# Another engine for the feature stores, a softmax taken in steps, a later swap of y, and four more gather buffers with a new pace in the routed stage of a PEER block

## The chip, the core and the metric

The kernel runs on one core of one Trainium2 chip. The metric is device time in microseconds (us) of one execution. A core has five engines, each with its own instruction stream, worked off in order: TensorE (PE, matrix products), VectorE (DVE), ScalarE (ACT), GpSimd (POOL) and SyncE (SP, which here only issues DMAs). Engines wait for each other by semaphores; DMA transfers are issued into a queue by one of the engines and move between HBM (DRAM) and the on-chip memories SBUF and PSUM.

## The reference, cut to what matters

The program is one layer of a hybrid decoder block for 256 tokens of width 2048: sparse attention and a convolution group side by side, an output projection, a residual with LayerNorm that gives y, and then a PEER mixer with 16384 experts, a second residual and a LayerNorm. The change lies in the PEER mixer:

```python
q = (yb @ wq).reshape(bsz, PEER_BLOCK, PEER_HEADS, 2, PK_HALF)
s1 = jnp.einsum('bthd,hkd->bthk', q[..., 0, :], sub_keys[:, 0])
s2 = jnp.einsum('bthd,hkd->bthk', q[..., 1, :], sub_keys[:, 1])
v1, i1 = lax.top_k(s1, PK_TOPK)
v2, i2 = lax.top_k(s2, PK_TOPK)
...
top, pos = lax.top_k(cand, PK_TOPK)
eidx = jnp.take_along_axis(cidx, pos, axis=-1)
g = jax.nn.softmax(top.astype(jnp.float32), axis=-1)
u = u_tab[eidx]
v = v_tab[eidx]
h = jax.nn.gelu(jnp.einsum('btd,bthkd->bthk', yb, u))
return jnp.einsum('bthk,bthkd->btd', g * h, v).astype(y.dtype)
```

Every token has 8 heads with 16 experts each, so 128 (head, rank) pairs a token, chosen among 128 x 128 experts (index = i1 * 128 + i2). `u_tab` and `v_tab` have 16384 rows of 2048 floats. For every pair the row of `u_tab` is multiplied with y, and the row of `v_tab` is added to the output with weight g * gelu(that product).

## The kernel before, in words

**Two ways to the same product.** The 256 tokens are two halves (tt = 0 and 1) of 128, one token on each partition. The columns of `u_tab` are split. The last 896 columns (`UG`) are fetched row by row: an indirect gather on GpSimd's queue (`gather_to`, L1168) brings, for one pair number c of one half, 128 rows of 896 floats, one for each token, and one VectorE instruction (`dot`, L1179) multiplies them with y and sums them into a column of `hv`. There are 256 such gathers, 128 for each half; `issued` counts gathers and `done` counts dots. The first 1152 columns (`UD`, nine chunks of 128) are computed densely: all 16384 experts are multiplied with y by TensorE, whichever are needed.

**The dense u loop (L1613 on).** Block j (of 128) takes 128 experts. `u_load` (L1208) has SyncE load them into one of four buffers `ur`. `u_split` makes two parts of them: ScalarE rounds them to the high part `uh` (L1232) and copies the first 768 columns to PSUM (`ut`, L1236); VectorE subtracts for the low part (L1237), GpSimd does it for the rest (L1238). `u_mult` is 27 matmuls on the block's transposed experts (high by high L1515, high by low L1516, low by high L1519) into one of two PSUM tiles, and `u_keep` (L1522) evicts these to `W[:, :, j]` by ScalarE. The loop body is an order written out by hand. For block j: the load for j + 4, the matmuls of j, the eviction of j - 1, the split of j + 2, then `dots_until`, which issues gathers up to a due count (at most two, `CATCH`, more than there were), and does the dots whose buffers it needs for them; then one step of `later_steps` (two, if the routing is behind the gathers).

**y and its swap.** The y that the dots read is a copy in PSUM, `yp`, of one half. When gather 128, the first of half 1, is about to be issued, `fetch` (L1489) reads y of half 1 into one of the gather buffers, by GpSimd's queue. The first `dot` of half 1 calls `swap` (L1495): ScalarE copies that buffer to `yp`.

**Routing in steps.** `later_steps` is a generator. It goes through the top-k selection of all heads, and then through `feature_steps`: for i1 and i2 VectorE makes four feature rows (`fr`: a constant, the index, and its square taken apart), each a bf16 tile of 128 x 256 in one of four scratch buffers, and ScalarE issues the ten stores that put them in DRAM (`feats`). Behind them stands the softmax of the gates, `gate_softmax`, once for each half: subtract (L1138, VectorE), exponent (L1139, ScalarE), sum, reciprocal and product (L1140 to L1142, VectorE). Two transposes by TensorE (L1562) and a copy give the gates' transposed form `gT`.

**The routed stage (L1652 to the v stage).** It picks, from `W`, the dense results for the experts that each token has chosen, and puts the weights back into `W` at the same places. A step q (of 64) does four tokens. Steps 0 to 35 go in pairs: `ext_hot` and `ext_mask` (L1660 and L1669, small matmuls from the stored features), a ReLU by ScalarE (`ext_relu`, L1665), four matmuls with `W` a step (`ext`, L1674; fp32, which the records count as eight), and a maximum by VectorE (`ext_max`, L1678). Steps 36 to 64 do one q each and also scatter block m = q - 37: `sc_hot`, `sc_relu`, `sc_val`, four matmuls `sc` (L1722) and `sc_keep`. The last 28 blocks are only scattered, in pairs. Around q = 32 the sums of half 0 are completed: `weight_sums` (after step 32), `weight_gelu` (ScalarE), `weight_gates` (L1693, VectorE, at step 34), and `weight_rows` (a transpose, L1653 in `to_cols`, into bank 4 and a copy, L1696, at step 36).

**Gathers and dots in the routed stage.** At its start 200 gathers were issued and 197 dots done. The other 56 go into spare buffers: three 896-column pieces of what held the transposed y (`more`), and the ring's three buffers as their dots are done. `x_dots(q, n)` is called behind each step's `ext`: gathers are issued up to the due count n; if no buffer is spare, the next dot is done. For every third dot (i % 3 == 1) the product alone goes to GpSimd (L1836), in place, and ScalarE sums it with an accumulating copy (`x_sum`, L1846) when a call at least two steps later comes to it; only then is the buffer spare again. In the last eight steps one more dot a step is done.

**After it** the v stage multiplies `W` with `v_tab`, dense and gathered in the same manner (L296 to L298 and L1745).

Of the kernel before, what the change touches and what calls it, by code (L numbers as in the profile page):

```python
# [8 lines left out]
F32 = mybir.dt.float32  # L9
# [4 lines left out]
AF = mybir.ActivationFunctionType  # L14
# [5 lines left out]
P = 128  # L20
# [59 lines left out]
def tile_hybrid_block(  # L80
# [1052 lines left out]
        for _ in route_steps(h, tt):  # L1133
            pass

    def gate_softmax(tt):
        sh = [P, PH, TOPK]
        nc.vector.tensor_tensor(gs[:, tt], top[:, tt], top[:, tt, :, 0:1].to_broadcast(sh), op=OP.subtract)  # L1138
        nc.scalar.activation(gs[:, tt], gs[:, tt], AF.Exp)  # L1139
        nc.vector.tensor_reduce(gsum[:, tt, :, 0], gs[:, tt], axis=AX.X, op=OP.add)  # L1140
        nc.vector.reciprocal(gsum[:, tt], gsum[:, tt])
        nc.vector.tensor_tensor(gs[:, tt], gs[:, tt], gsum[:, tt].to_broadcast(sh), op=OP.mult)  # L1142

    def fl(t, tt):
        return t[:, tt].rearrange("p a b -> p (a b)")
# [25 lines left out]

    def dot(i):
        tt, c = pairs[i]
        if yrow["tt"] is not None and yrow["tt"] != tt:
            yrow["swap"](tt)
        gt, ring = gts.pop(i)
        ring[2] -= 1
        yr = yg[:, tt, HC - UG:] if yrow["tt"] is None else yrow["at"]
        nc.vector.scalar_tensor_tensor(gt, gt, 1.0, yr, op0=OP.mult, op1=OP.mult,  # L1179
                                       accum_out=hv[:, tt, c:c + 1])  # L1180
# [31 lines left out]
    def dots_until(n, ending=10 ** 6):  # L1212
        nonlocal issued, done
        while issued < n:
            last = issued >= ending
            if issued == P:
                while rings[0][2] == rings[0][1]:
                    dot(done)
                    done += 1
                yrow["fetch"](1)  # L1220
            while room() == 0 or (last and rings[0][2] == rings[0][1]):
                dot(done)
                done += 1
            gather(issued, last)
            issued += 1
# [270 lines left out]
        rings[0][2] -= 1  # L1496
        yrow["tt"] = tt

    yrow["swap"], yrow["fetch"] = swap, fetch

    wpool = ctx.enter_context(ExitStack())
    wp = wpool.enter_context(tc.tile_pool(name="wp", bufs=1, reuse_waits="tile"))
# [25 lines left out]
    def feature_steps():  # L1528
        dump("i1", i1)
        dump("i2", i2)  # L1530
        for n, src in enumerate((i1, i2)):

            size = BIGM if n == 0 else 1.0
            v = src.rearrange("p a b c -> p a (b c)")
            sqf = tk.tile([P, 2, P], F32, name=f"fsq{n}", tag="oh", bufs=1)
            nc.vector.tensor_tensor(sqf, v, v, op=OP.mult)
            sqi = tk.tile([P, 2, P], U32, name=f"fsi{n}", tag="cand", bufs=1)
            nc.vector.tensor_copy(sqi, sqf)
            yield
            for f in range(4):  # L1540
                fr = tk.tile([P, 2, P], BF, name=f"fr{n}{f}", tag="scr", bufs=4)
                if f == 0:
                    nc.vector.memset(fr, size)
                elif f == 1:
                    nc.vector.tensor_scalar(fr, v, size, None, op0=OP.mult)
                else:
                    si = tk.tile([P, 2, P], U32, name=f"fi{n}{f}", tag="oh", bufs=1)
                    if f == 2:
                        nc.vector.tensor_scalar(si, sqi, 7, 7, op0=OP.logical_shift_right,
                                                op1=OP.logical_shift_left)  # L1550
                    else:
                        nc.vector.tensor_scalar(si, sqi, 127, None, op0=OP.bitwise_and)
                    nc.vector.tensor_scalar(fr, si, size, None, op0=OP.mult)
                yield
                for r in ((0, 1) if f == 0 else (f + 1,)):
                    nc.scalar.dma_start(feats[n][:, r].rearrange("a p c -> p a c"), fr)
        for tt in range(2):
            gate_softmax(tt)
            yield
        pt = psu.tile([P, UV], F32, name="colsg", tag="ut", bufs=2)  # L1560
        for tt in range(2):
            nc.tensor.transpose(pt[:, tt * P:(tt + 1) * P], fl(gs, tt), ident)  # L1562
        nc.scalar.activation(gT, pt[:, :T], AF.Copy)
        yield
# [47 lines left out]
    if True:  # L1612
        for j in range(P):  # L1613
            if j == P - 2:
                for _ in steps:
                    pass
                first_loads()
            upto = min(first + (rest - LATE) * (j + 1) // P + GAHEAD, 2 * P)
            if j + URB < P:
                u_load(j + URB)  # L1620
            u_mult(j)
            if j:
                u_keep(j - 1)
            if j + 2 < P:
                u_split(j + 2)
            dots_until(min(upto, routed, issued + CATCH), ending)
            next(steps, None)
            if routed < min(upto + 8, 2 * P):
                next(steps, None)
        for _ in steps:  # L1630
            pass
        assert not rings[1][2]
        rings.pop()
# [11 lines left out]

    xs = ctx.enter_context(ExitStack())
    px = xs.enter_context(tc.tile_pool(name="px", bufs=2, reuse_waits="tile"))

# [43 lines left out]

    def weight_rows(tt):
        nc.scalar.activation(wv[:, tt], to_cols(wT[:, tt * P:(tt + 1) * P], f"wvT{tt}",  # L1696
                                                more_banks[0] if tt else 4), AF.Copy)

    ohs, oas, pos = {}, {}, {}

# [130 lines left out]
    def x_dot(q):  # L1831
        nonlocal done
        i, done = done, done + 1
        gt, ring = gts[i]
        if i % 3 == XPOOL and i0 <= i < 2 * P - 4:
            nc.gpsimd.tensor_tensor(gt, gt, yx, op=OP.mult)  # L1836
            late.append((q, i))
            return
# [9 lines left out]

    def x_dots(q, n):
        nonlocal issued  # L1850
        while late and late[0][0] <= q - 2:
            x_sum()
        while issued < n:
            while not spare:
                if done < issued:
                    x_dot(q)
                else:
                    x_sum()
            gather_to(issued, spare.pop(0), [None, 0, 0])
            issued += 1  # L1860
        if q > NQ - 8 and done < issued:
            x_dot(q)

    manual = ctx.enter_context(ExitStack())
    manual.enter_context(tc.manual_schedule())
    if True:
        for q, hp in enumerate([ext_hot(q, True, 4) for q in range(2)]):
            ext_relu(q, hp, True)
        u_left = 2 * P - issued
        i0 = issued  # L1870

        def due(q):
            pace = q + 1 + PACE * max(0, q - LAG)
            return min(2 * P, i0 + -(-u_left * pace // (NQ - 4 + PACE * (NQ - 4 - LAG))))

        def loads(q):
            m = q - LAG
# [29 lines left out]
        for q in range(QP, NQ + 1):  # L1907
# [33 lines left out]
                sc_keep(m, sc(m) if q < NQ else sp)  # L1941
            if q == NQ:
                weight_gelu(1)
            if q == QP:
                weight_rows(0)
        for m in range(NQ - QP, NQ, 2):
            loads(m + LAG)
            loads(m + LAG + 1)
# [9 lines left out]
            sps = [sc(p, True) for p in (m, m + 1)]  # L1958
            for p, sp in zip((m, m + 1), sps):
                sc_keep(p, sp, p % 2 == 1)  # L1960
            if m == NQ - 12:
                v_raw(2)
                v_rows(0, 0)
# [5 lines left out]
            if m == NQ - QP + 4:  # L1969
                weight_rows(1)  # L1970
            if m == NQ - QP + 2:
                tks.close()
                upool.close()
                keep.close()
# [187 lines left out]
```

## Time and profile before

| | us |
|---|---|
| runs shown (3) | 1589.81, 1589.48, 1586.29 |
| median | 1589.48 |
| the profiled execution | 1588.19 |
| its span, first to last instruction | 1586.4 |

| stretch of the profiled execution | us | TensorE | VectorE | ScalarE | GpSimd | clock | DMA share |
|---|---|---|---|---|---|---|---|
| attention, convolution, y, query scores (0 to 507) | 507 | 499.30 | 393.09 | 269.18 | 228.56 | 1.00 | 0.59, then 0.70 |
| dense u loop (507 to 915) | 408 | 401.10 | 378.99 | 298.08 | 297.18 | 1.00 | 0.99 |
| routed stage, steps 0 to 64 (915 to 1038) | 123 | 113.82 | 104.82 | 79.09 | 94.11 | 0.94 | 0.75 |
| scatter alone (1038 to 1078) | 40 | 39.96 | 32.67 | 36.13 | 27.31 | 1.00 | 0.57 |
| v stage to the end (1078 to 1586) | 508 | 496.64 | 457.43 | 216.94 | 397.10 | 1.00 | 0.95 |

The columns of engines are busy times in us. "Clock" is the TensorE clock that the throttle granted, 1.00 being full speed, and "DMA share" is the mean busy share of the 16 DMA engines. The page of the profile lists groups of instructions by source line, with how often they ran, their mean time, how long the engine stood idle just before them, and which other engine's work ended that. `fr` is a feature row, `ur` a block of experts, `yp` y in PSUM, `gu`, `spare`, `moreh` and `morel` are gather buffers, `top` also holds the extracted activations `ha`, and `gs` the gates and later the weights. In a line with `->` or `<-` the part left of the arrow is written, and behind `<-` in brackets stands what the instruction waited for and for how long.

### The profile page before, as it was taken

The page shows a single profiled execution, that of the slowest core. Times are in us where ns is not written, and L with a number is a line of the kernel's source. Part 1 is how long each engine was busy: PE and PEld are TensorE (multiplying, and loading weights), DVE is VectorE, ACT ScalarE, POOL GpSimd, SP SyncE. Part 2 cuts the span into 40 slices and gives each one's busy share as a digit, 9 for nine tenths or more (in the row PEclk, how much of TensorE's full clock was granted, in tenths as well). Part 3 has the DMA queues.
Part 4 walks back from the last instruction along what each step waited for, and adds up shares of the span by engine and source line. Part 5 has one row for each costly group of instructions (what it writes and reads, how often), then busy time and mean ns, then how long its engine had stood idle before and what let it go on. Part 6 is the DMA issues. An engine that isn't in the chain of part 4 may idle for free.

```text
span 1586.4 us, 29450 instructions
## 1 busy us (share of the span) xinstructions
PE 1550.8 (98%) x10987; PEld 1435.9 (91%) x10987; DVE 1367.0 (86%) x2509; ACT 899.4 (57%) x1266; POOL 1044.3 (66%) x791
## 2 busy tenths in 40 slices
PE   9999999999999999999998999999999999999997
PEld 9999999988999999999998977788888888888886
DVE  6999777766578999999997788888999989989998
ACT  5345776645435777777776656785444444444443
POOL 1886000064887777777776677867888878878883
PEclk9999999999999999999999999999999999999999
DMA  9774455255867999999999886767999999999997
GB/s 299 239 231 147 139 161 184 92 207 182 258 209 272 397 382 393 383 390 384 387 388 366 304 276 216 235 196 247 346 368 355 356 371 346 357 376 355 366 356 248
DMA packets 161896, 466.59 MB, mean 294 GB/s; under 512 B 18304, under 2 KB 86424, under 8 KB 161496
## 3 DMA queue, kind: packets, MB, share of 16 engines
q1 hardware_dynamic: 117188, 261.95, 47.8%
q0 software_dynamic: 41040, 201.82, 34.5%
q8 instruction: 86, 1.41, 0.4%
q10 hardware_dynamic: 3524, 0.95, 0.3%
q14 instruction: 58, 0.48, 0.1%
HBM read 459.80 MB, written 4.85 MB: 293 GB/s over the span
## 4 chain that ended last, share of the span: by engine, by line
PE 83%; DVE 7%; DMA 3%; POOL 3%; issue 2%; ACT 2%; POOLq 0%; ACTq 0%; DVEq 0%
PE f L297 10%; PE f L298 10%; PE f L296 10%; PE hp L1515 8%; PE hp L1516 8%; PE hp L1519 7%; PE bank L1722 3%; DVE taps L492 2%; PE pwq L298 2%; PE pwq L297 2%; PE pwq L296 2%; PE bank L1674 2%; DMA feat<-fr 1%; PE mixa L296 1%; PE pcg L297 1%
## 5 line engine op out<-in xcount | busy, mean ns | idle before, releaser
L1745 POOL DMA_INDIRECT gv<-in_peer_v_dram,e x256 | 400.5, 1565 | 91.1 <-DVE gacc L1750 48.3
L1785 ACT ACTIVATE vh<-vr 128x1408 fp32r<-128x1408 f32 (+1 forms) x129 | 175.8, 1364 | 274.8 <-DVE gacc L1750 230.9
L297 PE MATMUL f<-vl,wh 128*128 128x512 f32 (+1 forms) x768 | 288.3, 375 | 1.7 <-DVE vl L1786 1.7
L296 PE MATMUL f<-vh,wh 128*128 128x512 f32 (+1 forms) x768 | 288.5, 376 | 0.0
L298 PE MATMUL f<-vh,wl 128*128 128x512 f32 (+1 forms) x768 | 288.1, 375 | 0.0
L1515 PE MATMUL hp<-yh,uh 128*128 128x256 f32 x1152 | 283.8, 285 | 4.2 <-ACT W L1522 4.2
L1516 PE MATMUL hp<-yl,uh 128*128 128x256 f32 x1152 | 283.4, 284 | 0.0
L257 POOL TENSOR_TENSOR lo<-raw,hi 128x1024 fp32r<-128x1024 f32 (+1 forms) x84 | 189.0, 2271 | 133.9 <-ACT hi L239 127.8
L1168 POOL DMA_INDIRECT gu<-in_peer_u_rows_dram,e x200 | 193.6, 968 | 117.9 <-DVE gu L1179 72.0
L1786 DVE TENSOR_TENSOR vl<-vr,vh 128x1408 fp32r<-128x1408 f32 (+1 forms) x129 | 206.5, 1602 | 41.3 <-ACT vh L1785 39.9
L1515 PEld LDWEIGHTS hp<-yh,uh 128*128 128x128 f32 x1152 | 222.5, 193 | 4.8 <-ACT W L1522 4.8
L1516 PEld LDWEIGHTS hp<-yl,uh 128*128 128x128 f32 x1152 | 222.6, 193 | 0.0
L1179 DVE SCALAR_TENSOR_TENSOR gu<-gu,yp 128x896 f32<-128x896 f32 x200 | 211.2, 1080 | 12.2 <-DMA gu<-in_peer_u_rows_dram,e 12.2
L239 ACT ACTIVATE hi<-raw 128x1024 fp32r<-128x1024 f32 (+1 forms) x137 | 141.2, 1036 | 141.0 <-PE pcg L297 29.1
L1750 DVE SCALAR_TENSOR_TENSOR gacc<-gv,hv,gacc 128x640 f32<-128x640 f32 x247 | 207.4, 880 | 2.9 <-DMA gv<-in_peer_v_dram,e 2.8
L1232 ACT ACTIVATE uh<-ur 128x1152 fp32r<-128x1152 f32 x128 | 149.6, 1168 | 95.6 <-issue 69.3
L297 PEld LDWEIGHTS f<-vl,wh 128*128 128x128 f32 x768 | 148.8, 194 | 22.9 <-DVE vl L1786 2.4
L296 PEld LDWEIGHTS f<-vh,wh 128*128 128x128 f32 x768 | 148.8, 194 | 20.7
L298 PEld LDWEIGHTS f<-vh,wl 128*128 128x128 f32 x768 | 149.0, 194 | 19.5
L1519 PE MATMUL hp<-yh,ul 128*128 128x256 f32 x1152 | 159.3, 284 | 0.0
L1519 PEld LDWEIGHTS hp<-yh,ul 128*128 128x128 f32 x1152 | 147.6, 192 | 0.1
L1237 DVE TENSOR_TENSOR ul<-ut,uh 128x768 fp32r<-128x768 f32 x126 | 119.9, 952 | 26.1 <-ACT ut L1236 23.2
(407 smaller groups left out, 3491.6 us busy)
## 6 DMA issues: line engine op xcount, KB each, us to landing
vr<-in_peer_v_dram SPq DMA_DIRECT2D x128, 704.0 KB
ur<-in_peer_u_dense_dram SPq DMA_DIRECT2D x128, 576.0 KB
raw<-in_w_in_dram SPq DMA_DIRECT2D x32, 1024.0 KB
raw<-in_w_out_dram SPq DMA_DIRECT2D x16, 1024.0 KB
raw<-in_peer_wq_dram SPq DMA_DIRECT2D x15, 1024.0 KB
gv<-in_peer_v_dram,e POOLq DMA_INDIRECT x256, 7.4
gu<-in_peer_u_rows_dram,e POOLq DMA_INDIRECT x200, 6.5
raw<-in_w_in_dram SPq DMA_DIRECT2D x4, 608.0 KB
```

The source lines that it names most:

```text
L257: e.tensor_tensor(lo[:, a:b], src[:, a:b], hi[:, a:b].bitcast(F32), op=OP.subtract)
L296: nc.tensor.matmul(acc, lhsT=ah, rhs=bh, start=start, stop=False)
L297: nc.tensor.matmul(acc, lhsT=ah, rhs=bl, start=False, stop=False)
L298: nc.tensor.matmul(acc, lhsT=al, rhs=bh, start=False, stop=stop)
L1168: nc.gpsimd.indirect_dma_start(out=gt, out_offset=None, in_=u_rows, in_offset=bass.IndirectOffsetOnAxis(ap=fl(e4, tt)[:, c:c + 1], axis=0))
L1179: nc.vector.scalar_tensor_tensor(gt, gt, 1.0, yr, op0=OP.mult, op1=OP.mult, accum_out=hv[:, tt, c:c + 1])
L1515: nc.tensor.matmul(hps[j], lhsT=uh[:, s], rhs=chunk(yh, k), start=k == 0, stop=False)
L1516: nc.tensor.matmul(hps[j], lhsT=uh[:, s], rhs=chunk(yl, k), start=False, stop=False)
L1519: nc.tensor.matmul(hps[j], lhsT=ul[:, s], rhs=chunk(yh, k), start=False, stop=k == UK - 1)
L1745: nc.gpsimd.indirect_dma_start(out=gvs[j, tt], out_offset=None, in_=v_tab, in_offset=bass.IndirectOffsetOnAxis(ap=fl(e4, tt)[:, j:j + 1], ...
L1750: engine.scalar_tensor_tensor(gacc[:, tt], gvs.pop((j, tt)), wv[:, tt, j:j + 1], gacc[:, tt], op0=OP.mult, op1=OP.add)
L1786: (nc.gpsimd if early else nc.vector).tensor_tensor(vl, src[:, s], vh.bitcast(F32), op=OP.subtract)
```

## The change

It has two parts.

In the dense u loop: the ten stores of the features are issued by SyncE instead of ScalarE. `gate_softmax` becomes a generator over both halves at once: a subtraction, two steps of pause, the exponent, one step of pause, then sum, reciprocal and product, and two more steps of pause before the transposes. `dot` no longer swaps y. `dots_until` returns when the dots of half 0 are all done and y hasn't been swapped; the swap is called in the loop body, behind the split of block j + 2 and ahead of `dots_until`.

In the routed stage: four more buffers of 896 columns (pool `gx`) are spare from the start, and are given back after the second pair of the last part. `x_dots` counts dots against the due count, not gathers; the count starts from the dots done (197) and is spread over nearly all 64 steps. All spare buffers are filled with gathers behind the dots of each call, as long as there are gathers left. The sum of a product is taken four steps after it instead of two. Products for GpSimd are counted in `owed`, and those that fall on steps 32 to 34 are put off to a later dot. The extra dot in the last eight steps goes. `weight_rows(0)` moves from step 36 to the second pair of the last part, and into bank 5.

```diff
-    def gate_softmax(tt):
-        sh = [P, PH, TOPK]
-        nc.vector.tensor_tensor(gs[:, tt], top[:, tt], top[:, tt, :, 0:1].to_broadcast(sh), op=OP.subtract)
-        nc.scalar.activation(gs[:, tt], gs[:, tt], AF.Exp)
...
+    def gate_softmax():
+        sh = [P, 2 * PH, TOPK]
+        g3, t3, s3 = (t.rearrange("p a b c -> p (a b) c") for t in (gs, top, gsum))
+        nc.vector.tensor_tensor(g3, t3, t3[:, :, 0:1].to_broadcast(sh), op=OP.subtract)
+        yield
+        yield
+        nc.scalar.activation(g3, g3, AF.Exp)
+        yield
+        nc.vector.tensor_reduce(s3[:, :, 0], g3, axis=AX.X, op=OP.add)
+        nc.vector.reciprocal(s3, s3)
+        nc.vector.tensor_tensor(g3, g3, s3.to_broadcast(sh), op=OP.mult)
+        yield
+        yield
...
     def dot(i):
         tt, c = pairs[i]
-        if yrow["tt"] is not None and yrow["tt"] != tt:
-            yrow["swap"](tt)
+        assert yrow["tt"] in (None, tt)
...
             while room() == 0 or (last and rings[0][2] == rings[0][1]):
+                if done == P and yrow["tt"] == 0:
+                    return
                 dot(done)
                 done += 1
...
                 for r in ((0, 1) if f == 0 else (f + 1,)):
-                    nc.scalar.dma_start(feats[n][:, r].rearrange("a p c -> p a c"), fr)
-        for tt in range(2):
-            gate_softmax(tt)
-            yield
+                    nc.sync.dma_start(feats[n][:, r].rearrange("a p c -> p a c"), fr)
+        yield from gate_softmax()
...
             if j + 2 < P:
                 u_split(j + 2)
+            if done == P and yrow["tt"] == 0:
+                swap(1)
             dots_until(min(upto, routed, issued + CATCH), ending)
...
+    gxs = ctx.enter_context(ExitStack())
+    gx = gxs.enter_context(tc.tile_pool(name="gx", bufs=1, reuse_waits="tile"))
+    spare.extend(gx.tile([P, UG], F32, name=f"gx{n}") for n in range(4))
...
     def weight_rows(tt):
         nc.scalar.activation(wv[:, tt], to_cols(wT[:, tt * P:(tt + 1) * P], f"wvT{tt}",
-                                                more_banks[0] if tt else 4), AF.Copy)
+                                                more_banks[0] if tt else 5), AF.Copy)
...
-        if i % 3 == XPOOL and i0 <= i < 2 * P - 4:
+        owed["n"] += i0 <= i < 2 * P - 4 and i % 3 == XPOOL
+        if owed["n"] and i0 <= i and not NQ // 2 <= q < NQ // 2 + 3:
+            owed["n"] -= 1
             nc.gpsimd.tensor_tensor(gt, gt, yx, op=OP.mult)
             late.append((q, i))
             return
...
     def x_dots(q, n):
         nonlocal issued
-        while late and late[0][0] <= q - 2:
+        while late and late[0][0] <= q - 4:
             x_sum()
-        while issued < n:
-            while not spare:
-                if done < issued:
-                    x_dot(q)
-                else:
+        while done < n:
+            while done == issued:
+                if not spare:
                     x_sum()
+                gather_to(issued, spare.pop(0), [None, 0, 0])
+                issued += 1
+            x_dot(q)
+        while spare and issued < 2 * P:
             gather_to(issued, spare.pop(0), [None, 0, 0])
             issued += 1
-        if q > NQ - 8 and done < issued:
-            x_dot(q)
...
-        u_left = 2 * P - issued
-        i0 = issued
+        u_left = 2 * P - done
+        i0, d0, owed = issued, done, {"n": 0}

         def due(q):
             pace = q + 1 + PACE * max(0, q - LAG)
-            return min(2 * P, i0 + -(-u_left * pace // (NQ - 4 + PACE * (NQ - 4 - LAG))))
+            return min(2 * P, d0 + -(-u_left * pace // (NQ - 1 + PACE * (NQ - 2 - LAG))))
...
-            if q == QP:
-                weight_rows(0)
...
+            if m == NQ - QP + 2:
+                weight_rows(0)
...
             if m == NQ - QP + 2:
+                gxs.close()
```

More of the change, by code (lines that the diff above doesn't have):

```diff
@@ L1134, in route @@
             pass
-    def gate_softmax(tt):
-        sh = [P, PH, TOPK]
[L1138 to L1142, printed above, removed]
+    def gate_softmax():
[11 more added lines that the diff above has]
+        yield
     def fl(t, tt):
@@ L1497, in swap @@
         yrow["tt"] = tt
-    yrow["swap"], yrow["fetch"] = swap, fetch
+    yrow["fetch"] = fetch
     wpool = ctx.enter_context(ExitStack())
```

## The prediction

> **What bounds the kernel now.** I read the page first, then the chain of waits over the expert half, then the waits and timelines of the places where that chain leaves TensorE.
>
> ```profile
> span 1586.4 us, 29450 instructions
> PE 1550.8 (98%) x10987; PEld 1435.9 (91%) x10987; DVE 1367.0 (86%) x2509; ACT 899.4 (57%) x1266; POOL 1044.3 (66%) x791
> PE 83%; DVE 7%; DMA 3%; POOL 3%; issue 2%; ACT 2%; POOLq 0%; ACTq 0%; DVEq 0%
> ```
>
> TensorE sets the end. The profiled execution took 1588.19 us (span 1586.4 and 1.8 around it), 0.1% under the median of the three runs, 1589.48. A gain can only come from the 17% of the chain that is not PE, and from matmuls slowed by waiting. The change touches two stages.
>
> In the dense u loop one block is 768+384 columns, 27 matmuls and one eviction W (L1522). The chain shows its period and two breaks:
>
> ```profile
> 735.59 1.08 PE hp L1519 x9
> 738.83 1.08 PE hp L1519 x9
> ...
> 759.95 1.08 PE hp L1519 x9
> ...
> 834.47 1.08 PE hp L1519 x9
> ...
> 839.27 17.17 DMA feat<-fr
> ...
> 874.76 1.08 PE hp L1519 x9
> ```
>
> The evictions of these two stretches, counted by stretch (columns: stretch, length, busy and count, clock, DMA share, GB/s):
>
> ```profile
> 738.83:759.95 21.12, 3.76 (x6) 1.00 0.99 365
> 834.47:874.76 40.29, 6.26 (x10) 0.96 0.99 361
> ```
>
> The undisturbed period is 738.83 - 735.59 = 3.24 us. The first stretch, with y's swap, lost 21.12 - 6 x 3.24 = 1.68 us; the second, with feature stores and the gates' softmax, 40.29 - 10 x 3.24 = 7.89. So 9.57 us is all that the edits in this loop can return. The waits that made them, ScalarE's and one of TensorE's:
>
> ```profile
> ACT yp L1495 <- DVE gu L1179: 1.8, 1, 1.8
> ACT W L1522 <- DMA feat<-fr: 5.3, 2, 3.6
> ACT gs L1139 <- DVE gs L1138: 3.7, 2, 3.3
> PE colsg L1562 <- DVE gs L1142: 2.5, 1, 2.5
> ```
>
> ScalarE is in order: each time it stands for a swap, a store or an exponent, the next high part and the eviction stand behind it, and TensorE stops.
>
> In the routed stage (L1674 rebuilds hidden activations, L1722 scatters weights) the period is that of the first two rows here; the others are its first pair, the pairs q = 32 and 34, and q = 63:
>
> ```profile
> 976.88 1.16 PE L1674 MATMUL bank<-W,slot 128*128 128x128 f32 x8
> 979.19 1.05 PE L1674 MATMUL bank<-W,slot 128*128 128x128 f32 x7
> ...
> 912.59 2.05 PE L1674 MATMUL bank<-W,slot 128*128 128x128 f32 x16
> 954.35 2.05 PE L1674 MATMUL bank<-W,slot 128*128 128x128 f32 x16
> 957.79 2.05 PE L1674 MATMUL bank<-W,slot 128*128 128x128 f32 x16
> 1034.63 1.16 PE L1674 MATMUL bank<-W,slot 128*128 128x128 f32 x8
> ```
>
> A pair of blocks (first half) and a block with a scatter (second) both want 2.31 us. 17 pairs took 45.20 where 39.27 would do, the 28 blocks after them 76.84 where 64.68 would do: 18.1 us lost. GpSimd is nearly as busy, by its products and gathers from 915.9 to 1031:
>
> ```profile
> 915.90:1031.00 115.10, 35.60 (x17) 0.94 0.76 240
> 915.90:1031.00 115.10, 54.53 (x57) 0.94 0.76 240
> ```
>
> and by the pitch of its queue:
>
> ```profile
> 919.53 0.95 POOL L1168 DMA_INDIRECT moreh<-in_peer_u_rows_dram,e  x1 [0.30 <-issue]
> 920.79 0.95 POOL L1168 DMA_INDIRECT morel<-in_peer_u_rows_dram,e  x1 [0.30 <-issue]
> ...
> 930.27 2.08 POOL L1836 TENSOR_TENSOR morel<-morel 128x896 f32<-128x896 f32 x1
> 932.51 0.98 POOL L1168 DMA_INDIRECT spare<-in_peer_u_rows_dram,e  x1 [0.16 <-DVE top L1678]
> ```
>
> A gather takes 1.25 us of the queue, a product 2.25: 57 x 1.25 + 17 x 2.25 = 109.5 of 115.1 us. TensorE's 18 us are therefore not all to be had.
>
> **The u loop, edit by edit.** *Swap.* The copy of 0.92 us moves behind the next block's high part, one step after the last dot that reads the old y, so its wait of 1.8 us is over before ScalarE comes to it.
>
> ```profile
> 756.02 0.92 ACT L1495 ACTIVATE yp<-yrow 128x896 f32<-128x896 f32 x1 [1.75 <-DVE gu L1179]
> 831.31 1.17 ACT L1232 ACTIVATE uh<-ur 128x1152 fp32r<-128x1152 f32 x1 [0.82 <-issue]
> 863.60 1.28 ACT L1139 ACT_TABLE_LOAD   x1 [0.91 <-DVE fr L1553]
> ```
>
> ScalarE idles 0.82 us a step, so 0.92 leaves about 0.1. VectorE's dots of that step, and the gathers that the early return puts off, wait behind the copy; catching up at two a step covers them. Gain 1.5, bounds 0.7 (the copy wholly uncovered) to 1.68.
>
> *Softmax.* One chain of five VectorE and ScalarE instructions on both halves replaces two; the exponent runs two steps after the subtraction and the reduction a step after that, the transposes two steps later. So 3.7 on ScalarE and 2.5 on TensorE go. The table load of 1.28 stays, with about 0.4 of exponent: 1.7 against 0.82 of slack, and two PSUM banks for the block's sums to carry the rest. I leave 0.3 us lost, bounds 0 and 0.9.
>
> *Stores.* Ten stores leave ScalarE, with the 5.3 us that it waited. SyncE now waits for each feature row; queued behind are the u loads, and ScalarE's high part waits for those.
>
> ```profile
> 834.60 0.33 SPq L1208 DMA_DIRECT2D ur<-in_peer_u_dense_dram  x1
> ...
> 836.15 0.41 DVE L1545 TENSOR_SCALAR fr<-i 128x256 bf16<-128x256 f32 x1
> ...
>   DMA ur<-in_peer_u_dense_dram: 0.9, 1
> ```
>
> A load that left at 834.60 would now leave behind a row ready at 836.56: 2 us late. Loads have that much in hand: of 128 high parts one waited for its load, 0.9 us (last row). I leave 1.0 us lost; its bounds are 0 and the price in the second rival.
>
> The loop: 1.68 - 1.5 = 0.18 and 1.3 of 7.89 stay, so 8.1 us are gained.
>
> **The routed stage.** Four more buffers mean that the queue on GpSimd no longer waits for a free one, but also that at q = 0 eight gathers are put into it at once instead of one. By the code's own order the first product (dot 202) stood behind 8 gathers since number 200 and was read by ScalarE (x_sum) at q = 13; now it stands behind 12 and is read at q = 11. The fifth product (214) stood behind 20 gathers and was read at q = 31; now 24, read at q = 29. From 919.53 (gather 201) the first product starts at 919.53 + 11 x 1.25 = 933.3 instead of 930.27; the fifth at 933.3 + 12 x 1.25 + 4 x 2.25 = 957.3, is done at 959.4, and with ScalarE's sum (1.1, estimated from the 896 columns of the copy above) the ReLU behind it feeds pair 32 at 961 instead of 954.35. ScalarE already stood for these products:
>
> ```profile
> ACT morel L1846 <- POOL morel L1836: 5.1, 2, 2.7
> ```
>
> The longer lag (four q instead of two) doesn't cover it, since the product is issued four to five q earlier in the order too. Dots 197 and 198 also come ahead of the first reductions on VectorE, which already waited for a gather:
>
> ```profile
> 916.92 1.09 DVE L1179 SCALAR_TENSOR_TENSOR gu<-gu,yp 128x896 f32<-128x896 f32 x1 [2.37 <-DMA gu<-in_peer_u_rows_dram,e]
> ```
>
> That is 2 to 3 us more for TensorE at the third pair, but inside the hold just worked out.
>
> At the turn to the second half three waits lie together:
>
> ```profile
> 959.07 2.22 DVE L1693 TENSOR_TENSOR gs<-top,i 128x128 f32<-128x128 f32 x1 [1.04 <-ACT top L1689]
> ...
> 959.04 2.09 POOL L1836 TENSOR_TENSOR moreh<-moreh,morel 128x896 f32<-128x896 f32 x1
> ...
> 963.97 0.47 PE L1653 MATMUL bank<-ident,gs 128*128 128x128 f32 x1 [2.42 <-DVE top L1678]
> ```
>
> The gate product on VectorE lasted just as long as GpSimd's product beside it; no product is issued at q = 32 to 34 now, and the transposes of L1653 move to the last part, where they cost TensorE the same 0.3 to 0.5 us. So 2.42 goes; the Gelu's table load (1.28 as above) and the sum of dot 217 stay ahead of q = 36 on ScalarE, which I put at 968. From there GpSimd is ahead: by the order of the code every product is done before its sum, so 27 blocks at 2.31 end at 1030.4. I add 2 us for slow matmuls behind the remaining stops: 1032.4 against 1034.63, a gain of 2.2. Bounds: GpSimd's floor, 915.9 + 109.5 = 1025.4 and a sum and a block after it, 1027.5 (7.1 gained); and the 6.6 of pair 32 kept to the end (6.6 lost). I take 2.2, from the row of the queue.
>
> The 2 us are from this row, the stretch with the stop of 2.42:
>
> ```profile
> 960.00:970.00 10.00, 7.39 (x38) 5.09 (x36) 7.09 (x11) 3.98 (x9) 6.10 (x5) 0.66 0.65 214
> ```
>
> The granted clock was 0.66 in it. [...]
>
> **Sum.** 1588.19 - 8.1 - 2.2 = 1577.9; I forecast 1578 for the median. The runs differ by 3.5 us among themselves, so 0.2% (3.2 us) is what a measurement can tell from no change: faster is under 1586.3, slower over 1592.7.
>
> **Rivals.** *GpSimd is no hold (0.20).* If ScalarE comes to the sums late enough, TensorE follows GpSimd's floor: 7.1 in the stage and 9 in the loop give 1572. For it: GpSimd waited for buffers before, and these waits are what the change removes. Against: the order puts more gathers ahead of each product.
>
> *Stores starve the loads (0.15).* [...]
>
> *The hold lasts (0.18).* The first half's 6.6 us is not made up: 1588.2 - 8.1 + 6.6 = 1586.7, and 1590 with another 3 us of slow clock.
>
> **How the numbers follow.** Forecast 0.47, between 1573 and 1583. Faster: 0.47 + 0.20 + 0.08 of the third rival = 0.75. Same: 0.06 of the second and 0.07 of the third. Slower: 0.09 and 0.03 = 0.12. The range runs from below the GpSimd floor, 1569, to 1590, which leaves out most of the starved loads and the tail of the best case.
>
> **What would show it.** In the changed profile the u loop has no break near 751 or 850 longer than 0.5 us, no ScalarE wait for feat, and the high parts wait for ur under 2 us in all. In the routed stage gathers follow each other at 1.25 without waits for dots, products start later than before up to q = 30 and earlier after q = 38, and L1674 is behind before's at q = 32 and ahead at q = 63. I am wrong if ScalarE doesn't wait for the products at all, if ur is waited for by more than 5 us, or if the gain lies in neither stage.

## The result

| | median us | ratio to before [95% interval] |
|---|---|---|
| kernel before, 6 runs | 1589.64 | |
| the change, 6 runs | 1580.76 | 0.9946 [0.9933, 0.9958] |

The change makes the kernel 0.54% faster, 8.9 us in the medians. The forecast was 1578.0 and the case behind it 1573 to 1583. The profiled execution of the change took 1580.19 us, 8.0 less than that of before. Its page:

```profile
span 1578.4 us, 29466 instructions
PE 1547.6 (98%) x10987; PEld 1433.3 (91%) x10987; DVE 1363.7 (86%) x2505; ACT 898.4 (57%) x1265; POOL 1041.5 (66%) x791
PE 86%; DVE 6%; DMA 2%; issue 2%; POOL 2%; ACT 1%; POOLq 0%; SPq 0%; DVEq 0%; ACTq 0%
```

TensorE is still what ends last; its share of the chain rose from 83 to 86%, and VectorE, the DMAs and GpSimd gave up the rest. Where the 8.0 us lie is read from four stretches that begin and end with the same instructions in both kernels: the six blocks of the u loop with y's swap, the fifteen blocks with the features and the softmax, and the routed stage from step 0 to 36 and from 36 to 63. The columns are the stretch, its length, TensorE's busy time and count, its clock, DMA share and GB/s. First before, then the change:

```profile
738.66:759.78 21.12, 19.87 (x164) 1.00 0.99 364
834.30:890.79 56.49, 51.02 (x409) 0.97 0.96 346
912.59:960.39 47.80, 44.49 (x362) 1.00 0.85 273
960.39:1034.63 74.24, 68.73 (x534) 0.91 0.71 225
```

```profile
738.59:759.67 21.08, 19.83 (x164) 1.00 0.95 356
834.19:885.02 50.83, 49.21 (x410) 1.00 1.02 390
906.82:962.45 55.63, 47.46 (x362) 0.91 0.85 282
962.45:1026.22 63.77, 63.41 (x534) 0.97 0.70 223
```

The swap's six blocks are as long as before (six periods of 3.24 are 19.44). The fifteen blocks lost 56.49 - 15 x 3.24 = 7.89 us and lose 50.83 - 48.60 = 2.23 now. The routed stage first falls back by 55.63 - 47.80 = 7.8 us and then makes up 74.24 - 63.77 = 10.5. So 5.7 us come from the loop and 2.6 from the stage, and what follows takes 0.4 longer.

**The swap.** ScalarE's row of it in the changed kernel:

```profile
755.90 0.92 ACT L1502 ACTIVATE yp<-yrow 128x896 f32<-128x896 f32 x1 [1.75 <-DVE gu L1184]
```

It is the row of before with other line numbers, 1.75 us of wait and all. In ScalarE's order of instructions the copy stands where it stood, behind the same `ut` and ahead of the same eviction.

**Stores and softmax.** No wait of ScalarE for a feature or for the subtraction is left. Its waits for u loads, 0.9 us before, are these now, and the rows after them are where TensorE's last break begins:

```profile
ACT uh L1239 <- DMA ur<-in_peer_u_dense_dram: 7.6, 6, 1.9
```

```profile
861.86 1.17 ACT L1239 ACTIVATE uh<-ur 128x1152 fp32r<-128x1152 f32 x1 [1.92 <-DMA ur<-in_peer_u_dense_dram]
...
865.32 1.17 ACT L1239 ACTIVATE uh<-ur 128x1152 fp32r<-128x1152 f32 x1 [1.03 <-DMA ur<-in_peer_u_dense_dram]
...
867.20 1.28 ACT L1142 ACT_TABLE_LOAD   x1
868.50 0.42 ACT L1142 ACTIVATE gs<-gs 128x256 f32<-128x256 f32 x1
```

Two late loads use up ScalarE's slack, the table load and the exponent come on top, and TensorE loses 1.87 us at block 117 and 0.35 at block 119.

**The routed stage.** VectorE at the third pair, then TensorE:

```profile
911.44 1.09 DVE L1184 SCALAR_TENSOR_TENSOR gu<-gu,yp 128x896 f32<-128x896 f32 x1 [2.17 <-DMA gu<-in_peer_u_rows_dram,e]
...
913.44 1.09 DVE L1184 SCALAR_TENSOR_TENSOR gu<-gu,yp 128x896 f32<-128x896 f32 x1 [0.91 <-DMA gu<-in_peer_u_rows_dram,e]
```

```profile
916.34 1.18 PE L1679 MATMUL bank<-quad,fext 20*128 20x512 bf16 x2 [4.84 <-DVE top L1688]
```

The dots that are now due from step 0 wait for gathers that the loop issued late; the maxima behind them on VectorE hold the banks (of PSUM, into which TensorE writes), and TensorE stops for 6.0 us against 2.4 before. At step 14 it stops again, for the first product:

```profile
927.80 0.95 POOL L1174 DMA_INDIRECT moreh<-in_peer_u_rows_dram,e  x1 [0.30 <-DVE gx L1184]
928.77 2.10 POOL L1848 TENSOR_TENSOR morel<-morel 128x896 f32<-128x896 f32 x1
...
930.90 0.95 ACT L1858 ACTIVATE morel<-morel 128x896 f32<-128x896 f32 x1 [3.93 <-POOL morel L1848]
```

At the turn to the second half the gate product on VectorE, which took 2.22 us in before beside a product of GpSimd, is short with none beside it:

```profile
961.14 0.29 DVE L1703 TENSOR_TENSOR gs<-top,i 128x128 f32<-128x128 f32 x1 [1.13 <-ACT top L1699]
```

From step 38 on there is no stop left: the 25 steps from 38 (at 968.50) to 63 (at 1026.22) take 57.72 us, 25 periods of 2.31.

### The profile page after: what moved, and what is told of

The parts are those of the page before. It is cut to its first block, busy times and chain, and to the rows that moved or that the text cites. A ratio compares the mean times of both kernels' runs of the same rounds, so it can differ in the third digit from the quotient of the medians.

```text
span 1578.4 us, 29466 instructions
## 1 busy us (share of the span) xinstructions
PE 1547.6 (98%) x10987; PEld 1433.3 (91%) x10987; DVE 1363.7 (86%) x2505; ACT 898.4 (57%) x1265; POOL 1041.5 (66%) x791
## 4 chain that ended last, share of the span: by engine, by line
PE 86%; DVE 6%; DMA 2%; issue 2%; POOL 2%; ACT 1%; POOLq 0%; SPq 0%; DVEq 0%; ACTq 0%
PE f L297 10%; PE f L298 10%; PE f L296 10%; PE hp L1522 8%; PE hp L1523 8%; PE hp L1526 8%; PE bank L1732 3%; PE bank L1684 3%; DVE taps L492 2%; PE pwq L298 2%; PE pwq L297 2%; PE pwq L296 2%; PE mixa L296 1%; DMA ur<-in_peer_u_dense_dram 1%; PE pcg L297 1%
```

## The experiments

All runs are read with the same four stretches. "Lost" is the stretch less its periods. The stretches are those of one profiled execution of each kernel, those of before and of the change as above. The first four ran on one chip, the next four on a second, the last four on a third; the kernel before took 1594.5, 1588.4 and 1589.4 us there, and the ratios are to it.

| kernel | ratio [95% interval] | swap lost | features lost | steps 0 to 36 | steps 36 to 63 |
|---|---|---|---|---|---|
| before | 1 | 1.68 | 7.89 | 47.80 | 74.24 |
| the change | 0.9946 [0.9933, 0.9958] | 1.64 | 2.23 | 55.63 | 63.77 |
| e1 loop's edits alone | 0.9972 [0.9955, 0.9988] | 1.64 | 3.68 | 51.83 | 73.76 |
| e2 stage's edits alone | 1.0052 [1.0029, 1.0075] | 1.76 | 7.47 | 58.02 | 69.15 |
| e3 stores on ScalarE | 1.0028 [1.0009, 1.0046] | 1.64 | 0.56 | 59.58 | 67.76 |
| e4 swap later | 1.0019 [0.9998, 1.0041] | 0.13 | 6.04 | 58.97 | 68.65 |
| e5 the change again | 0.9935 [0.9909, 0.9961] | 1.64 | 3.52 | 55.39 | 63.78 |
| e6 aged rows | 0.9935 [0.9916, 0.9955] | 1.83 | 1.05 | 55.27 | 62.19 |
| e7 late dots | 0.9912 [0.9886, 0.9937] | 1.66 | 2.03 | 51.28 | 62.85 |
| e8 fewer products | 0.9942 [0.9924, 0.996] | 1.64 | 2.88 | 56.06 | 62.11 |
| e9 stage's edits alone | 0.9957 [0.994, 0.9973] | 1.64 | 11.05 | 55.40 | 61.93 |
| e10 late dots, swap, ScalarE | 0.9914 [0.9881, 0.9946] | 0.14 | 3.87 | 50.95 | 62.96 |
| e11 late dots, swap, aged rows | 0.9886 [0.9855, 0.9917] | 0.13 | 1.04 | 50.83 | 62.83 |
| e12 no buffers | 0.9954 [0.9942, 0.9966] | 1.63 | 1.31 | 50.82 | 69.97 |

**The two halves of the change, e1, e2 and e9.** e1 is before with the loop's edits, e2 and e9 are one kernel: the change with these undone.

```diff
...
-                    nc.sync.dma_start(feats[n][:, r].rearrange("a p c -> p a c"), fr)
-        yield from gate_softmax()
+                    nc.scalar.dma_start(feats[n][:, r].rearrange("a p c -> p a c"), fr)
+        for tt in range(2):
+            gate_softmax(tt)
+            yield
...
-            if done == P and yrow["tt"] == 0:
-                swap(1)
...
```

> The kernel before with the loop's edits alone (stores by SyncE, softmax in steps, the swap's call in the loop); the routed stage as before. Theory A (the two halves of the change add up): the loop's blocks 0 to 127 take 5.8 us less than before, the routed stage takes 122.0 us from its first to its last group of L1674 as before, and the time is 1589.6 - 5.8 = 1583.8, ratio 0.9964. Rival (the gathers, not TensorE, set when the routed stage ends, so a loop that ends sooner only waits longer there): the routed stage takes 125 to 128 us and the time is 1587 to 1590.

> The kernel after with the loop's edits undone; the routed stage as after. Theory A: the loop shows before's stops at blocks 112, 115 and 116 (3.6, 1.3 and 3.0 us), the routed stage takes 119.4 us from first to last group where before's took 122.0, and the time is 1589.6 - 2.6 = 1587.0, ratio 0.9984. Rival (the stage's gain comes from how the dots stand when the loop ends, which the loop's edits changed): the stage takes 122 us and the time is 1589.6.

e1 gives 0.28%, with 4.2 us won in the feature stretch. Its ratio lies between theory A's 0.9964 and the rival's (1587 us of 1589.6 are 0.998); its routed stage takes 125.6 us, which is the rival's figure. Whether the loop's edits or this chip made the stage 3.5 us longer is not shown: before wasn't profiled on this chip, and e1 lost 2.9 us at steps 10 and 12, near where the other kernels of this chip stop. e2 fell out of both: slower than before by 0.5%. Its stage lost in places where no wait of the program explains it; no such row stands in the profiles of before, the change and e1:

```profile
DVE top L1681 <- remote: 9.3, 2, 6.8
```

"remote" stands for a semaphore that rose without an instruction in the profile that ended then. It is TensorE's semaphore for which VectorE waited here, while TensorE's own records show small holes without a cause. e3 and e4, on the same chip, have the same stops (at steps 8, 10, 47 and 56). So the same kernel ran once more, on the third chip:

> The stage's edits alone once more, unaltered, beside a kernel before that runs anew. Theory A (the two halves add up, and what made the first try slow was the state of that chip, where TensorE also stood still in stretches that no wait explains): the routed stage takes 119 to 120.5 us from first to last group and the ratio is 0.997 to 0.9995. Rival (the stage's edits need the loop's): the stage takes 126 us or more again, ratio 1.003 to 1.006.

```profile
915.79:971.19 55.40, 47.32 (x362) 0.91 0.86 284
971.19:1033.12 61.93, 61.81 (x534) 1.00 0.72 228
```

The rival fell. Theory A held in its direction and was too cautious: 117.3 us for the stage where it had 119 to 120.5, and a ratio of 0.9957 where it had 0.997 or more, although the loop's breaks were 3 us longer in this execution than in before's profile. With e1's 0.28% the halves make 0.7%, within their intervals the change's 0.54 to 0.65. What TensorE lacked on the first chip stays open; the routed stages of e2, e3 and e4 are not used below.

**The stores, e3 and e6.** e3 gives the stores back to ScalarE and keeps the softmax in steps:

```diff
-                    nc.sync.dma_start(feats[n][:, r].rearrange("a p c -> p a c"), fr)
+                    nc.scalar.dma_start(feats[n][:, r].rearrange("a p c -> p a c"), fr)
```

> The kernel after with the ten stores issued by ScalarE again; the softmax stays in steps. Theory A (the stores on ScalarE cost the stop at block 112, and their being on SyncE costs the late loads behind the stop at block 117): block 112 loses 3.6 us again, blocks 117 and 119 lose under 1 instead of 2.2, high parts wait for their loads under 1 us instead of 7.6, and the time is 1580.8 + 3.6 - 1.4 = 1583.0. Rival (the stop at 117 is the exponent and its table load alone, late loads do nothing): 117 still loses 1.9 and the time is 1580.8 + 3.6 = 1584.4.

```profile
834.23:883.39 49.16, 49.16 (x409) 1.00 1.02 402
```

```profile
ACT W L1529 <- DMA feat<-fr: 1.0, 1, 1.0
```

The rival fell: blocks 117 and 119 lost 0.2 and 0.35 us. Theory A held in that half, for no high part waited for its load any more; but the stop at block 112 didn't come back. The fifteen blocks lost 0.56 us, a quarter of what the change loses. A store waited here at the head of ScalarE until an earlier store had landed, as the row shows, in which the eviction W stands behind such a store. In this execution that one had landed 12.5 us after its issue, and ScalarE stood for 1.0 us; in before's it took 15.9, and ScalarE stood for 3.6. e6 keeps SyncE and issues each store a step later:

```diff
                 yield
-                for r in ((0, 1) if f == 0 else (f + 1,)):
-                    nc.sync.dma_start(feats[n][:, r].rearrange("a p c -> p a c"), fr)
+                aged.append((n, f, fr))
+                if len(aged) > 1:
+                    put(*aged.pop(0))
```

> The kernel after with each feature store issued one step later, so that its row is ready when SyncE comes to it. Theory A (the loads are late because SyncE waits for rows ahead of them): loads leave up to 2 us sooner, the high parts wait for their loads under 3 us instead of 7.6, the stop at block 117 falls from 1.9 to under 0.6, the loop takes 1.5 to 2 us less. Rival (the loads are late because they land in 8 to 9 us instead of 5 to 6 while stores and gathers share their engines): the waits and the stop stay as they are, the loop within 0.4 us of the change's.

SyncE in the change, then in e6: a load leaves right behind a store that waited for its row, or ahead of it.

```profile
836.48 0.36 SPq L1563 DMA_DIRECT2D feat<-fr  x1
836.95 0.49 SPq L1213 DMA_DIRECT2D ur<-in_peer_u_dense_dram  x1
```

```profile
835.17 0.34 SPq L1213 DMA_DIRECT2D ur<-in_peer_u_dense_dram  x1
836.81 0.36 SPq L1542 DMA_DIRECT2D feat<-fr  x1
```

Both theories have a part. The loads that stood behind a store leave 1.0 to 2.9 us sooner for their block, and 1.05 us is lost in place of 2.23 and, in e5, 3.52. But the loads still land late (8.2 us on the mean of the fourteen around the stores, 7.6 in the change, 6.8 in before), and the high parts still wait 6.0 us for them. The rest, 0.85 at block 120, are TensorE's two transposes of the gates and their wait of 0.42 for a bank. The size is loose: the change's own loop ran also in e1, e5, e7, e8 and e12 and lost 1.3 to 3.7 us there, so e6 wins 0.3 to 2.6, and the medians of e5 and e6, 1579.15 and 1578.59 us, don't tell the two apart.

**The swap, e4.**

```diff
             if done == P and yrow["tt"] == 0:
-                swap(1)
+                if yrow.setdefault("old", j) < j:
+                    swap(1)
```

> The kernel after with the swap called one block later than the first block that finds half 0's dots done. In the trace of the change the copy still stands directly behind the same high part on ScalarE as before, and waits 1.75 us for the last dot. Theory A (the copy was moved nowhere, because VectorE runs one block behind): one block later the dot is done, ScalarE's wait for it falls from 1.75 to under 0.3, the stop of 1.51 us at block 83 to under 0.3, and the time is 1580.8 - 1.3 = 1579.5. Rival (the copy itself and the dots held behind it make the stop): the stop only moves to block 84, with 1 to 2 us, and the time stays at 1580.8 or rises by up to 1.

```profile
738.57:758.14 19.57, 19.57 (x165) 1.00 0.96 352
```

```profile
756.96 0.90 ACT L1502 ACTIVATE yp<-yrow 128x896 f32<-128x896 f32 x1
```

Theory A held for the stop: no wait, no break. In the changed kernel VectorE is one block behind, so the copy that the code calls one step after the last dot came to ScalarE ahead of that dot. The time itself was made by the other stops on this chip: u loads kept the high parts waiting for 20.1 us in this execution.

**The change once more, e5.**

> The changed kernel itself, unaltered, beside the kernel before and beside the next three. In the first four runs every kernel with the new routed stage needed 127 us from the first to the last group of L1684, where the profile of the change needed 119.4. Theory A (that was the other chip or its state, and those edits did no harm to the stage): here too the changed kernel's stage takes 126 us or more if the kernel before takes 1594, and its ratio is over 0.998. Rival (the stage is 119 us wherever the change runs whole, and it was the edits of those runs that cost 8 us): stage 119 to 121, ratio 0.994 to 0.996.

The rival's numbers came: 119.2 us for the stage, 0.65% faster. Its reason, that the edits of e2 to e4 cost the 8 us, did not hold: e9 is e2's kernel, and its stage took 117.3 us on the third chip. So the 127 us belong to the first chip or to its state, which these runs can't tell apart.

**The early dots, e7.**

```diff
-            pace = q + 1 + PACE * max(0, q - LAG)
-            return min(2 * P, d0 + -(-u_left * pace // (NQ - 1 + PACE * (NQ - 2 - LAG))))
+            pace = max(0, q + 1 - 4) + PACE * max(0, q - LAG)
+            return min(2 * P, d0 + -(-u_left * pace // (NQ - 1 - 4 + PACE * (NQ - 2 - LAG))))
```

> The kernel after with the due count of the routed stage starting four steps later (the dots of the first four steps come later, all gathers as soon as there is a buffer). Theory A (GpSimd's queue sets the pace, TensorE's first stop is hidden behind its product): the stop of 6.0 us at the third pair falls under 2.5, the later stops grow by as much, and step 63 comes within 1 us of the change's. Rival (the early stop is a loss of its own): step 63 comes 3 to 4 us sooner.

```profile
906.84:958.12 51.28, 46.79 (x362) 0.93 0.87 287
958.12:1020.97 62.85, 62.08 (x533) 1.00 0.76 239
```

The rival held, and more: step 63 comes 5.0 us sooner in its stage than in e5's (114.1 against 119.2). The third pair's stop fell from 5.6 to 2.8 and the slow pair behind it went; at the first product, now at steps 18 to 22, TensorE lost 5.4 us where e5 lost 4.5 at 14 to 18, and the smaller stops from 32 to 38 fell from 3.7 to under 1. The early stop was a loss of its own, which GpSimd's queue did not take back. The four runs of e7 (1574.65 to 1575.58 us) all lie below the four of e5 (1577.75 to 1580.85) on the same chip.

**Fewer products, e8.**

```diff
-        owed["n"] += i0 <= i < 2 * P - 4 and i % 3 == XPOOL
+        owed["n"] += i0 <= i < 2 * P - 4 and i % 4 == XPOOL
```

> The kernel after with every fourth dot's product on GpSimd instead of every third (13 instead of 17); four more whole dots on VectorE. Theory A (GpSimd is the limit of the first half of the stage: 57 gathers at 1.25 and 17 products at 2.25 are 109.5 us of it): GpSimd's work falls by 9 us, the stops at steps 14 to 18 and 32 to 38 (8 us together) fall by half or more, step 63 comes 3 to 5 us sooner. Rival (VectorE is as tight): its dots come ahead of the maxima, TensorE waits for banks, step 63 comes at the same time or up to 3 us later.

```profile
930.29 0.95 ACT L1858 ACTIVATE moreh<-moreh 128x896 f32<-128x896 f32 x1 [5.23 <-POOL moreh L1848]
```

Step 63 comes 1.0 us sooner in its stage, not 3 to 5: theory A fell in its size, and the rival's "same time or later" with it. The stops at 32 to 38 went, all but 0.5 us, but the first product stands behind as many gathers as ever, its sum comes a step or two earlier, and TensorE lost 6.9 us there. What held the first half was the place of the first product, not the number of products; e12, below, moves that place. Fewer products together with late dots were not run.

**No added buffers, e12.**

```diff
-    spare.extend(gx.tile([P, UG], F32, name=f"gx{n}") for n in range(4))
+    spare.extend(gx.tile([P, UG], F32, name=f"gx{n}") for n in range(0))
```

> The kernel after without its four added gather buffers; the pace, the lag of the sums and the held products stay. Theory A (the buffers let the gathers run ahead, and GpSimd waits for a free one without them): the second half's stops come back, the stage takes 122 us or more in place of 119.3, the time rises by 2.7 or more. Rival (the pace and the lag of the sums make the gain; the buffers put four more gathers ahead of the first product and hold TensorE there): the stops at steps 14 to 18 shrink, the stage takes 116 to 119 us, and the time is the change's or up to 3 us less.

```profile
922.56 2.10 POOL L1848 TENSOR_TENSOR morel<-morel 128x896 f32<-128x896 f32 x1
```

```profile
982.82 1.09 DVE L1184 SCALAR_TENSOR_TENSOR spare<-spare,yp 128x896 f32<-128x896 f32 x1 [3.17 <-DMA spare<-in_peer_u_rows_dram,e]
```

Neither theory's figure came, 120.8 us lying between 119 and 122, but each is right about one half of the stage. Without the buffers the first product starts 5.2 us sooner after the stage's first group (16.7 against 21.9) and the first half takes 4.8 us less; later the dots wait for gathers that no longer run ahead, and the second half takes 6.2 us more. The buffers are worth the difference, 1.4 us in these two profiles, which the ratios (0.9954 and 0.9946, with intervals that overlap) don't show. The stop at the third pair stays, at 5.5 us, so it is the pace that makes it and not the buffers; and the stops at steps 37 and 38, 5.0 us in before, are gone without them. No run takes out alone the products held back there, the moved transposes or the longer lag of the sums.

**Put together, e10 and e11.** Both have e7's late dots and e4's later swap; e10 has e3's stores on ScalarE, e11 e6's aged rows.

> The kernel after with three edits: the dots of the routed stage start four steps later, the swap is called one block later, and ScalarE issues the stores again (the softmax stays in steps). Theory A (the stores did no good on SyncE's queue, the swap's stop is a wait for the last dot, the early dots cost TensorE 4 us): the loop loses 0.5 to 1.5 us against its period in place of 3.9, the routed stage takes 114 us, and the time is 2 to 3 us under the 1575.1 of the kernel with late dots alone, 1572.5. Rival (the stores land in 15 us as in the profile of before, and ScalarE waits for an earlier one's landing again): the loop loses 4 us or more, and the time is 1575 to 1577.

> The kernel after with three edits: late dots, the swap one block later, and the stores on SyncE but one step later, behind a row that is ready. Theory A: the loop loses 1.2 to 2.2 us, the stage takes 114 us, the time is 1573 to 1574, 1 us over the kernel with ScalarE's stores. [...]

For e10 the rival held, 1575.43 us. ScalarE in it:

```profile
847.78 4.14 ACTq L1563 DMA_DIRECT2D feat<-fr  x2
851.97 0.60 ACT L1529 ACTIVATE W<-hp 128x256 f32<-128x256 f32 x1 [4.42 <-DVE fr L1552]
```

It stood between two stores until an earlier one, issued at 834.77, had landed at 851.53. That store landed in 16.8 us where e3's took 12.5: with the stores on ScalarE the fifteen blocks lost 0.56 us in e3 and 3.87 in e10, as the landing fell. For e11 theory A held (1.2 us lost in the loop, 113.7 in the stage) with a time under its range. It gave the lowest time of all, 1571.29 us, ratio 0.9886, which is below before and the change; towards e7 and e10 the intervals overlap, though its four runs (1571.02 to 1572.00) lie below all of e10's on the same chip (1574.82 and more). Its four stretches:

```profile
738.65:758.22 19.57, 19.57 (x164) 1.00 0.96 357
832.84:882.48 49.64, 49.22 (x409) 1.00 1.02 402
904.28:955.11 50.83, 46.33 (x362) 0.97 0.87 289
955.11:1017.94 62.83, 62.08 (x533) 1.00 0.76 239
```

The edits' gains add: 1.5 us at the swap, 1.2 at the features and 5.7 in the stage against the change's profile, 8.4 in all, where e4, e6 and e7 alone had 1.5, 1.2 and 5.3; the medians differ by 9.5.

## Why the prediction was right, and where its steps failed

The time came out within the forecast's case, 2.8 us above its figure, by two steps that fell short and one that gave more. That the stage's figure was so close is in part luck, as its way there was another.

- **The swap, 1.5 forecast, none found.** The step that failed is that the copy "moves behind the next block's high part, one step after the last dot". The code says so and the instruction order doesn't show it: in before, too, the first dot of half 1 was the first call of its block. I counted in blocks of the code where VectorE's lag decides. e4 shows that the price of the wait was right.
- **Stores and softmax, 1.3 left of 7.89 forecast, 2.23 found (3.52 in e5).** The mechanism was right: SyncE waits for rows, loads leave 2 us late (block 111's at 836.95, in before at 834.60), the table load of 1.28 comes on top. The term was too small, its upper bound, the price in the second rival, is shown by no run, and one sign that I named as proof of error came: the high parts waited 7.6 us for loads, more than 5, of which TensorE lost only 2.2. The gain that I gave to the stores is not theirs alone: e3 shows that with the softmax in steps they could stay on ScalarE for 0.56 us, and e10 that they could not always.
- **The starved loads.** The second rival has the stores on SyncE's queue delay the loads by enough to leave no gain or a loss; how much was an estimate of mine, which no run shows. The loads around the stores landed 0.8 us later on the mean (7.6 against 6.8), so that rival fell. In before a load left 8.9 us ahead of its high part and landed in 6.8 (medians of blocks 60 to 107), so that 2 us were in hand. The stores themselves landed after 3.2 to 17.2 us in before, issued by ScalarE, and after 4.5 to 6.5 in the change, issued by SyncE behind the loads; what makes the difference, no run takes apart.
- **The routed stage, 2.2 forecast, 2.6 found.** The turning points were well placed, each from the stage's first group: the fifth product 44.7 forecast and 45.0 found, step 32 48.4 and 49.5, step 36 55.4 and 55.6, step 63 119.8 and 119.4. The way there was not the one I gave. I put the hold at the fifth product and the third pair's stop "inside" it; TensorE lost 7.4 us at that pair and the next and 4.4 at the first product, and by the fifth there was nothing left to hold. e7 shows that the first of these was not covered by the second. At the turn the forecast held: the gate product fell from 2.22 to 0.29 us, and the wait of 2.42 for the transpose is gone.
- **The second half** ran at its period from step 38, as forecast. Once the ring's last gathers were out, the gathers did go 1.25 us apart but for one wait of 3.4, and e12, where two of them in the second half wait 1.8 again, shows that it is the buffers that do this. Of the 2 us kept for slow matmuls 1.6 came, at step 38, with the granted clock at 0.50 from 964.8 to 968.2.
- **GpSimd's floor.** The first rival's 7.1 us in the stage would be 114.9 us; e7, e10 and e11 reach 114.1, 113.9 and 113.7 with the same 57 gathers and 17 products. So it was about right, some 1 us too high, and the change stood 5 us above what these reach. In e11 the queue is the limit: from 911 to 1014, nearly the whole of its stage, GpSimd never stands for more than 0.3 us, the gap that lies between any two of its gathers, where in before it stood for up to 3.9. The first row of its waits there in e11, and the row of its longest wait in before:

```profile
POOL gx L1174 <- issue: 4.5, 18, 0.3
```

```profile
POOL morel L1168 <- DVE morel L1179: 3.9, 1, 3.9
```

## What to carry to other kernels

A move in the code is a move only if the engine's own order of instructions changes (y's copy waited 1.75 us before its call was moved and 1.75 after): compare the two orders, and count an engine's lag, before pricing it. More buffers let a queue run ahead, and what is queued behind the run, here a product that another engine waits for, starts later (21.9 us after the stage's first group with the four buffers, 16.7 without); pace the first steps of a stage separately from the rest (which gave 5.0 us in e7). An instruction that waits at the head of a queue, such as a store for its row, should be issued when its input is already there (in e6 the fifteen blocks lost 1.05 us, in the runs of the change's own loop 1.3 to 3.7).

## What the hardware showed that I had not expected

TensorE's granted clock fell to 0.50 seven times ahead of the last matmul, in before at 853.9, 963.2, 1000.7 and 1024.6, in the change at 913.6, 934.1 and 964.8, for 6.8 us at 963.2 and 913.6 and for 3.4 us at the others. In the change, what came ahead of a fall and the slow stretch behind it, twice (columns as above, the clock behind the count; the first stop had lasted 2.1 us by then and went on into the slow stretch), and once in e11:

```profile
911.10:913.60 2.50, 0.40 (x3) 1.00 0.73 247
913.62:920.42 6.80, 4.07 (x16) 0.50 0.79 248
930.20:934.08 3.88, 1.49 (x11) 1.00 0.92 323
934.10:937.50 3.40, 3.40 (x19) 0.50 0.73 225
```

```profile
907.80:911.18 3.38, 1.75 (x12) 1.00 0.70 215
911.20:914.60 3.40, 3.40 (x16) 0.50 0.80 237
```

Ahead of these three falls TensorE was without matmuls for 2.1 of 2.5 us, 2.4 of 3.9 and, in e11, 1.6 of 3.4. Not every such stop had a fall behind it: e10 stood for 1.8 us at the same place as e11, and its next pair took 2.05 us where e11's took 3.62. The sixteen matmuls of the next pair in e10 and in e11:

```profile
913.84 2.05 PE L1685 MATMUL bank<-W,slot 128*128 128x128 f32 x16
```

```profile
911.27 3.62 PE L1694 MATMUL bank<-W,slot 128*128 128x128 f32 x16
```

What decides between the two is not shown. With a fall behind it a stop cost more than itself: the pair that followed took another 1.4 us in the change and 1.6 in e11; in e10, with no fall there, nothing.

The same 64 KB store landed in 4.5 to 6.5 us on the queue of the loads in the change, in up to 10 in e6 and e11, and in up to 19 on a queue of its own in e9. And one kernel's routed stage took 127.2 us on one chip (e2) and 117.3 on another (e9), with no wait that tells why.
